# A float32 transformer block on one core: the same program with its SBUF operands moved apart modulo 512 bytes

## The chip, the cores and the metric

The kernel runs on one core of one Trainium2 chip. The metric is the device time of one execution in microseconds (us), as the median of several; smaller is better. Before the change the median of three executions is 741.97 us (741.67 to 742.17).

## The reference

The program is one layer of a streaming encoder for 512 frames of 1024 features, all in float32:

```
hn    = rms_norm(x) * norm1_g
proj  = hn @ w_in                      # [q_A k_A v_A | q_B k_B v_B | g_A g_B], 5120 wide
o_A   = softmax attention, 8 heads x 64, QK-norm, relative bias, all keys up to the frame's own 64-frame chunk
o_B   = stick-breaking attention, 8 heads x 64, strictly causal, no softmax
x     = x + (sigmoid(g_A) * (o_A @ w_branch_a) + sigmoid(g_B) * (o_B @ w_branch_b)) @ w_out
hid   = conv3(rms_norm(x) * norm2_g @ w_ffn_up) + conv_b     # causal, depthwise, 2 x 2816 wide
x     = x + (silu(hid[:, :2816]) * hid[:, 2816:]) @ w_ffn_down
```

## The kernel before

**Split products.** Every large product is made from two halves of each operand in the type that the profile calls fp32r: a high half (the cast of the number) and a low half (number minus high half). A product of two operands then takes three matmuls on TensorE: high by high, low by high and high by low. In the projections these are lines 188, 189 and 190 (`mm3`), in the first two projections line 306, in the down-projection lines 880, 881 and 882. Each matmul is two records in the profile: a weight load (PEld, 128x128, the stationary operand) and the matmul proper (PE, 256 or 512 columns of the moving operand). A row such as `pg<-hth,whi_up` names the output, then the moving operand, then the stationary one.

**Chunks of weights.** All weights of the projections come from HBM in chunks of 1 MB (128 partitions of 8 KB), those of the down-projection in chunks of 512 KB. `load` starts a chunk's transfer on the SP queue, into the tile `raw`, which has two places. `split_gen` then casts it on ScalarE into the tile `whi` (line 161) and subtracts on VectorE into the tile `wlo` (line 163); both tiles have two places too, so that chunk i+1 is split while TensorE works on chunk i (`run_chunk`). When a chunk is split, its raw place is free, and the chunk after the next is asked for at that point.

**The stages.** First the inputs and the first weights arrive and x is scaled and split into `hth` and `htl` (the transposed activations, 8 x 512 columns each); then the 24 projection chunks run with the two attentions between them; then the product with `w_out` and the second norm; then 22 up-projection chunks (48 matmuls of 512 columns each, in the first two chunks twice as many of 256; stationary `whi_up` or `wlo_up`, moving `hth` or `htl`), behind which the convolution, the gate and `pair_sums` prepare the down-projection's operands. The down-projection is a Strassen-like scheme of 7 products for each of 11 pairs of feature tiles and each half of the output columns. Its stationary operands are the 11 tiles `a`, eight of which lie in eight places with the tag `ap`; its moving operands are 256-column blocks of the weights' halves. Late weight chunks (`hl`) and the rows of x that are added at the end (`x_0`, `x_1`) take over places of `ap` whose operand is done.

**What sets the order.** The order of instructions on each engine is fixed when the program is built; engines wait for one another by semaphores. Tiles get fixed addresses at that time: each pool lays its places one behind the other along a partition, so the length of a tile decides where everything behind it begins.

**Where operands begin before.** In the program as built every matmul operand begins at a multiple of 512 bytes along its partition, with the one exception of a small column of row norms (line 280).

Of the kernel before, what the change touches and what calls it, by code (L numbers as in the profile page):

```python
# [8 lines left out]
F32 = mybir.dt.float32  # L9
F32R = mybir.dt.float32r  # L10
# [5 lines left out]
P = 128  # L16
S = 512
D = 1024
NT = S // P
# [45 lines left out]
def block_kernel(ctx: ExitStack, tc: tile.TileContext, x, xt, params, g2, rbx, wts, wdn, out):  # L65
# [6 lines left out]
    wp = ctx.enter_context(tc.tile_pool(name="wp", bufs=2))  # L72
# [30 lines left out]
    order = [key for key, _, _ in CHUNKS]  # L103

    raws, splits, late, ring = {}, {}, {}, []
    FIRST_DN = order.index("dn0_0")

    def load(i, parts=1):
        if i >= FIRST_DN:

            j = (i - FIRST_DN) % 3
            if i in (FIRST_DN, FIRST_DN + 2):
                ring.append(wp.tile([P, 2048], F32, tag="raw", name=f"raw_dn{len(ring)}"))
            raws[i] = ring[j // 2][:, j % 2 * 1024:(j % 2 + 1) * 1024]
            SP.dma_start(raws[i], wdn[i - FIRST_DN])
            yield
            return
        raws[i] = wp.tile([P, 2048], F32, tag="raw", name=f"raw_{order[i]}")
        n = 2048 // parts
        for j in range(parts):  # L120
            SP.dma_start(raws[i][:, j * n:(j + 1) * n], wts[i, :, j * n:(j + 1) * n])
            yield

    def down_sums(raw):

        b = raw.rearrange("p (b c) -> p b c", c=256)
        ts = ring[1][:, 1024:2048]
        t = ts.rearrange("p (b c) -> p b c", c=256)
        V.tensor_tensor(t[:, 0:2], b[:, 0:4:2], b[:, 0:2][:, ::-1], op=ALU.subtract)
        V.tensor_tensor(t[:, 2], b[:, 2], t[:, 0], op=ALU.subtract)  # L130
        ins = V.tensor_tensor(t[:, 3], t[:, 2], b[:, 3], op=ALU.subtract)

        late["halves"] = late.get("halves", ()) + (ins,)
        return ts

    def split_gen(i, pieces):

        if i >= len(order):
            return
        key = order[i]  # L140
        kn = CHUNKS[i][1]
        raw = raws.pop(i)
        if i < FIRST_DN + NP + 5:
            hi = wp.tile([P, 2048], F32R, tag="whi", name=f"whi_{key}")
            lo = wp.tile([P, 2048], F32R, tag="wlo", name=f"wlo_{key}")
        n = 2048 // pieces
        cuts = [(n * j, raw[:, n * j:n * (j + 1)]) for j in range(pieces)] if i < FIRST_DN else []
        if i >= FIRST_DN:

            if i < FIRST_DN + NP + 5:  # L150
                hi, lo = hi[:, 0:1792], lo[:, 0:1792]
            else:
                hl = late["pool"].tile([P, 3584], F32R, tag="ap", name=f"hl_{key}", bufs=8)
                hi, lo = hl[:, 0:1792], hl[:, 1792:3584]
            cuts, kn = [(0, raw[:, 256:1024]), (768, down_sums(raw))], 7
        splits[key] = (hi.rearrange("p (k c) -> p k c", k=kn), lo.rearrange("p (k c) -> p k c", k=kn))

        nxt = [i + 2] if i + 2 < FIRST_DN else [i + 2, i + 3] if i + 2 == FIRST_DN else [i + 3]
        for j, (o, src) in enumerate(cuts):
            sl = slice(o, o + src.shape[-1])  # L160
            cast = A.copy(hi[:, sl], src)  # L161
            E = G if i == 2 else V
            ins = E.tensor_tensor(lo[:, sl], src, hi[:, sl].bitcast(F32), op=ALU.subtract)  # L163
            if i >= FIRST_DN:

                late["halves"] = (behind(ins, late.get("halves", ())),)
                late["casts"] = (behind(cast, late.get("casts", ())),)
            if j == len(cuts) - 1:
                for n in nxt:
                    if n < len(order):  # L170
                        next(load(n))
            yield
# [3 lines left out]
    def run_chunk(key, body, pieces=4):  # L176

        sp = split_gen(pos[key] + 1, pieces)
        hi, lo = splits.pop(key)
        for _ in body(hi, lo):  # L180
            next(sp, None)
            yield
        for _ in sp:
            pass
# [29 lines left out]


    first = load(0, NK)
    for k in range(NK):
        SP.dma_start(xs[:, k, :], xt[k])
        next(first)
    for _ in load(1, 4):  # L220
        pass
# [31 lines left out]
    g1 = par[:, C_G1:C_G1 + NK]  # L253

    sp0 = split_gen(0, NK)
    for k in range(NK):
        A.activation(hth[:, k, :], xs[:, k, :], AF.Copy, scale=g1[:, k:k + 1])
# [284 lines left out]
    def behind(ins, others):  # L542

        for o in others:
            tc.add_manual_dep(ins.ins, o.ins.name, mybir.DependencyInfo(
                mybir.DependencyClass.NoSync, mybir.DependencyReason.DATA), reason="table order")
        return ins
# [104 lines left out]
    for s in range(len(steps)):  # L652
# [6 lines left out]
        br, h, t, e = pend.pop(0)  # L659
# [95 lines left out]
    hi, lo = splits.pop("wo3")  # L755
    sp = iter(())
    for y in wo_body(3)(hi, lo):
        if y == "split":
            sp = split_gen(pos["up0"], 4)
        next(sp, None)  # L760
# [3 lines left out]
    fp = late["pool"] = ctx.enter_context(tc.tile_pool(name="fp", bufs=1))  # L764
# [29 lines left out]
    def pair_sums(i):  # L794

        u0, u1 = ub[:, 2 * i % 4, :], ub[:, 2 * i % 4 + 1, :]
        lo_, hi_ = slice(0, 256), slice(256, 512)
        st = fp.tile([P, 768], F32, tag="st", name=f"st{i}", bufs=1)
        V.tensor_tensor(st[:, 0:256], u0[:, hi_], u1[:, hi_], op=ALU.add)
        V.tensor_tensor(u0[:, hi_], u0[:, lo_], u0[:, hi_], op=ALU.subtract)  # L800
        V.tensor_tensor(st[:, 256:512], st[:, 0:256], u0[:, lo_], op=ALU.subtract)
        V.tensor_tensor(st[:, 512:768], u1[:, lo_], st[:, 256:512], op=ALU.subtract)
        if i < 8:
            a = fp.tile([P, 3584], F32R, tag="ap", name=f"a{i}", bufs=8)
        else:
            a = cp.tile([P, 4096], F32R, tag=("xs", "hth", "htl")[i - 8], name=f"a{i}")
        pairs[i] = a
        for src, o, n in ((u0, 0, 512), (u1, 512, 512), (st, 1024, 768)):
            A.copy(a[:, o:o + n], src)
            V.tensor_tensor(a[:, 1792 + o:1792 + o + n], src, a[:, o:o + n].bitcast(F32), op=ALU.subtract)  # L810

    def up_fin(j, pg, pu, g=None):
        if g is None:
            g = gate(j, pg)
        u = ub[:, j % 4, :]
        conv(pu, NF + j, u)
        V.tensor_tensor(u, g, u, op=ALU.mult)
        if j % 2 == 1 and j // 2 < 9:
            pair_sums(j // 2)
# [29 lines left out]
    for i in (9, 10):  # L849
        pair_sums(i)  # L850
# [34 lines left out]
    def add(o, a, b, op=ALU.add, after=()):  # L885
        return behind(V.tensor_tensor(o, a, b, op=op), after)

    def blk(x, r, c):

        return x[:, 2 * r:2 * r + 2, 256 * c:256 * (c + 1)]  # L890
# [1 line left out]
    v3 = lambda ap: ap.rearrange("p (t c) -> p t c", t=2)  # L892

    def fetch(name, col):
        x = fp.tile([P, 3584], F32, tag="ap", name=name, bufs=8)[:, 0:2048].rearrange("p (t c) -> p t c", t=NT)
        for t in range(NT):
            SP.dma_start(x[:, t, :], x2d[t, :, col:col + 512])
        return x
# [22 lines left out]
    def rest0():  # L921

        c, u, v = tmp["c"], tmp["u"], tmp["v"]
        x = fp.tile([P, 3584], F32, tag="ap", name="x_0", bufs=8)[:, 0:2048].rearrange("p (t c) -> p t c", t=NT)
        get = lambda t: SP.dma_start(x[:, t, :], x2d[t, :, 0:512])
        for t, (o, i) in enumerate(((v3(u), blk(c, 1, 1)), (blk(c, 0, 1), v3(v)),
                                    (blk(c, 1, 1), v3(v)), (blk(c, 1, 0), v3(u)))):
            get(t)
            add(o, o, i, after=late["halves"])
            yield  # L930
        for t in range(NT):
            add(c[:, t, :], c[:, t, :], x[:, t, :], after=late["halves"])
            SP.dma_start(out[0, t * P:(t + 1) * P, 0:512], c[:, t, :])
            yield
# [49 lines left out]
    for s in range(2):  # L984
        for i in range(NP - 2 * s):
            if (s, i) == (0, 6):
                tmp["c"] = fp.tile([P, NT, S], F32, tag="ub", name="c_0")
            if (s, i) == (1, 1):
                rest = rest0()
            for _ in run_chunk(f"dn{s}_{i}", down_body(s, i)):  # L990
                pass

    for _ in split_gen(pos[f"dn1_{NP - 1}"], 2):
        pass
    tmp["x"] = fetch("x_1", 512)
    ends = [(i, splits.pop(f"dn1_{i}")) for i in (NP - 2, NP - 1)]
    prev = ()
# [54 lines left out]
```

## Time and profile before

| what | value |
|---|---|
| median of three executions | 741.97 us (741.67 to 742.17) |
| the profiled execution's own time | 742.19 us |
| its span, first to last instruction | 740.5 us |
| granted TensorE clock | 1.000 |
| TensorE busy, matmuls | 733.9 us, 4301 records |
| TensorE busy, weight loads | 651.9 us |
| VectorE, ScalarE, GpSimd busy | 538.0, 377.6 and 41.8 us |
| read from and written to HBM | 75.07 and 4.19 MB |

The span leaves 1.69 us of the profiled execution's own time outside (742.19 less 740.5). Busy times of PE overstate its work, since a matmul's record overlaps the next one's; how fast TensorE really goes is read from the distance between the starts of matmuls that follow one another, called pitch below.

### The profile page before, as it was taken

Reading aid. Unit: us, or ns where it says so; the run is one execution under the profiler, and the core shown is the slowest. Engines: PE = TensorE matmul, PEld = TensorE weight load, DVE = VectorE, ACT = ScalarE, POOL = GpSimd, SP = SyncE. Lnnn points to the kernel's source line nnn. Section 1 sums busy time; section 2 is a strip of 40 time slices with the busy share of each in tenths; the row PEclk is TensorE's granted clock in tenths of the full one; section 3 lists DMA queues with packets and bytes.
Section 4 is the critical chain, followed back from the end, with each engine's and each line's share of the span. In section 5 each row is a group of like instructions: output and inputs, shape, how many; then the busy total and the mean of one; then the engine's idle time right before and its main releaser. Section 6 shows DMA issues by size and latency. Waiting matters only on the chain.

```text
span 740.5 us, 10983 instructions
## 1 busy us (share of the span) xinstructions
PE 733.9 (99%) x4301; PEld 651.9 (88%) x4301; DVE 538.0 (73%) x984; ACT 377.6 (51%) x674; POOL 41.8 (6%) x73
## 2 busy tenths in 40 slices
PE   9999999999999999999999999999999999999997
PEld 8999998888988888888899888888888888999997
DVE  6578876775887888385275876766777676978895
ACT  6675655557766686353153554445355434434430
POOL 2701200000101111000000000000000000000000
PEclk9999999999999999999999999999999999999999
DMA  8632232211222112224332312322331321232552
GB/s 307 247 121 81 77 114 72 72 58 62 111 86 85 58 58 107 93 88 197 143 146 80 144 62 110 114 80 91 113 106 66 113 86 58 86 114 92 168 168 88
DMA packets 19205, 79.98 MB, mean 108 GB/s; under 512 B 2128, under 2 KB 4304, under 8 KB 13008
## 3 DMA queue, kind: packets, MB, share of 16 engines
q1 hardware_dynamic: 18864, 79.04, 30.5%
q8 instruction: 34, 0.56, 0.3%
q10 hardware_dynamic: 288, 0.23, 0.1%
q14 instruction: 19, 0.16, 0.1%
HBM read 75.07 MB, written 4.19 MB: 107 GB/s over the span
## 4 chain that ended last, share of the span: by engine, by line
PE 98%; DMA 1%; ACT 0%; DVE 0%; issue 0%; SPq 0%; DVEq 0%
PE pg L189 5%; PE pu L188 5%; PE pg L188 5%; PE pu L189 5%; PE pu L190 5%; PE pg L190 5%; PE P L882 5%; PE P L881 5%; PE P L880 5%; PE gA L188 2%; PE qkB L188 2%; PE gA L189 2%; PE gB L190 2%; PE qkB L190 2%; PE gB L188 2%; PE gA L190 2%
## 5 line engine op out<-in xcount | busy, mean ns | idle before, releaser
L163 DVE TENSOR_TENSOR wlo_up<-raw_up,whi_up 128x1024 fp32r<-128x1024 f32 (+1 forms) x50 | 52.4, 1094 | 49.4 <-ACT whi_up L161 49.4
L190 PE MATMUL pg<-hth,wlo_up 128*128 128x512 f32 (+1 forms) x192 | 71.5, 372 | 0.0
L189 PE MATMUL pu<-htl,whi_up 128*128 128x512 f32 (+1 forms) x192 | 71.5, 372 | 0.0
L188 PE MATMUL pg<-hth,whi_up 128*128 128x512 f32 (+1 forms) x192 | 71.4, 372 | 0.0
L188 PE MATMUL pu<-hth,whi_up 128*128 128x512 f32 (+1 forms) x192 | 71.4, 372 | 0.0
L189 PE MATMUL pg<-htl,whi_up 128*128 128x512 f32 (+1 forms) x192 | 71.4, 372 | 0.0
L190 PE MATMUL pu<-hth,wlo_up 128*128 128x512 f32 (+1 forms) x192 | 71.4, 372 | 0.0
L881 PE MATMUL P<-wlo_dn,a 128*128 128x256 f32 x224 | 62.2, 284 | 0.0
L882 PE MATMUL P<-whi_dn,a 128*128 128x256 f32 x224 | 62.1, 283 | 0.0
L880 PE MATMUL P<-whi_dn,a 128*128 128x256 f32 x224 | 59.1, 284 | 0.5 <-ACT whi_dn L161 0.5
L161 ACT CAST whi_up<-raw_up 128x1024 fp32r<-128x1024 f32 (+1 forms) x50 | 44.6, 948 | 29.2 <-PE pu L189 25.5
L161 ACT CAST whi_dn<-raw_dn 128x768 fp32r<-128x768 f32 (+1 forms) x32 | 29.0, 941 | 37.3 <-issue 22.3
L163 DVE TENSOR_TENSOR wlo_dn<-raw_dn,whi_dn 128x768 fp32r<-128x768 f32 (+1 forms) x32 | 34.8, 1091 | 15.1 <-ACT whi_dn L161 15.0
L881 PEld LDWEIGHTS P<-wlo_dn,a 128*128 128x128 f32 x224 | 43.1, 192 | 0.0
L882 PEld LDWEIGHTS P<-whi_dn,a 128*128 128x128 f32 x224 | 43.0, 192 | 0.0
L880 PEld LDWEIGHTS P<-whi_dn,a 128*128 128x128 f32 x224 | 41.0, 192 | 1.0 <-ACT whi_dn L161 0.9
L188 PEld LDWEIGHTS pu<-hth,whi_up 128*128 128x128 f32 x192 | 36.2, 189 | 6.3
L188 PEld LDWEIGHTS pg<-hth,whi_up 128*128 128x128 f32 x192 | 36.2, 189 | 6.3
L190 PEld LDWEIGHTS pu<-hth,wlo_up 128*128 128x128 f32 x192 | 36.2, 189 | 6.3
L190 PEld LDWEIGHTS pg<-hth,wlo_up 128*128 128x128 f32 x192 | 36.2, 188 | 6.3
L189 PEld LDWEIGHTS pu<-htl,whi_up 128*128 128x128 f32 x192 | 36.2, 189 | 6.1
L189 PEld LDWEIGHTS pg<-htl,whi_up 128*128 128x128 f32 x192 | 36.2, 189 | 6.1
(260 smaller groups left out, 2073.6 us busy)
## 6 DMA issues: line engine op xcount, KB each, us to landing
raw_up<-in_wts SPq DMA_DIRECT2D x22, 1024.0 KB, 4.7
raw_dn<-in_wdn SPq DMA_DIRECT2D x22, 512.0 KB, 3.3
raw_gA<-in_wts SPq DMA_DIRECT2D x4, 1024.0 KB, 4.7
raw_qkB<-in_wts SPq DMA_DIRECT2D x4, 1024.0 KB, 4.8
raw_gB<-in_wts SPq DMA_DIRECT2D x4, 1024.0 KB, 4.7
raw_wo<-in_wts SPq DMA_DIRECT2D x4, 1024.0 KB, 4.8
xs<-in_xt SPq DMA_DIRECT2D x8, 256.0 KB, 4.6
xtok<-in_x SPq DMA_DIRECT2D x4, 512.0 KB, 7.7
```

The source lines that it names most:

```text
L161: cast = A.copy(hi[:, sl], src)
L163: ins = E.tensor_tensor(lo[:, sl], src, hi[:, sl].bitcast(F32), op=ALU.subtract)
L188: PE.matmul(ps, sh, mh, start=first, stop=False)
L189: PE.matmul(ps, sh, ml, start=False, stop=False)
L190: PE.matmul(ps, sl, mh, start=False, stop=last)
L880: behind(PE.matmul(dst, sh, mh, start=first and t == 0, stop=False, skip_group_check=True), prev)
L881: PE.matmul(dst, sh, ml, start=False, stop=False, skip_group_check=True)
L882: prev = (PE.matmul(dst, sl, mh, start=False, stop=last, skip_group_check=True),)
```

## The change

Tiles are made longer than what they hold; the added bytes are never read or written. `raw` grows by 32 bytes per partition and place, `whi` and `wlo` by 64, the `ap` places by 64. All the slices that the program uses keep their lengths. The order of instructions on all engines, and the semaphores that they wait for, are the same in both built programs, row for row.

| tile | begins, bytes modulo 512, before | after |
|---|---|---|
| `raw`, two places | 0, 0 | 0, 32 |
| `whi`, two places | 0, 0 | 64, 128 |
| `wlo`, two places | 0, 0 | 192, 256 |
| `hth`, `htl`, `xs` (and the tiles that take their places) | 0 | 320 |
| tiles of the two attentions: `q`, `k`, `v`, probabilities, identity | 0 | 320 |
| `ap`, eight places | 0 (all) | 320, 256, 192, 128, 64, 0, 448, 384 |

```
-                ring.append(wp.tile([P, 2048], F32, tag="raw", name=f"raw_dn{len(ring)}"))
+                ring.append(wp.tile([P, 2056], F32, tag="raw", name=f"raw_dn{len(ring)}"))
...
-        raws[i] = wp.tile([P, 2048], F32, tag="raw", name=f"raw_{order[i]}")
+        raws[i] = wp.tile([P, 2056], F32, tag="raw", name=f"raw_{order[i]}")[:, 0:2048]
...
-            hi = wp.tile([P, 2048], F32R, tag="whi", name=f"whi_{key}")
-            lo = wp.tile([P, 2048], F32R, tag="wlo", name=f"wlo_{key}")
+            hi = wp.tile([P, 2064], F32R, tag="whi", name=f"whi_{key}")[:, 0:2048]
+            lo = wp.tile([P, 2064], F32R, tag="wlo", name=f"wlo_{key}")[:, 0:2048]
...
-                hl = late["pool"].tile([P, 3584], F32R, tag="ap", name=f"hl_{key}", bufs=8)
+                hl = late["pool"].tile([P, 3600], F32R, tag="ap", name=f"hl_{key}", bufs=8)
...
-            a = fp.tile([P, 3584], F32R, tag="ap", name=f"a{i}", bufs=8)
+            a = fp.tile([P, 3600], F32R, tag="ap", name=f"a{i}", bufs=8)
...
-        x = fp.tile([P, 3584], F32, tag="ap", name=name, bufs=8)[:, 0:2048].rearrange("p (t c) -> p t c", t=NT)
+        x = fp.tile([P, 3600], F32, tag="ap", name=name, bufs=8)[:, 0:2048].rearrange("p (t c) -> p t c", t=NT)
```

The two `x` lines (in `fetch` and in `rest0`) change alike.

More of the change, by code (lines that the diff above doesn't have):

```diff
@@ L923, in rest0 @@
         c, u, v = tmp["c"], tmp["u"], tmp["v"]
-        x = fp.tile([P, 3584], F32, tag="ap", name="x_0", bufs=8)[:, 0:2048].rearrange("p (t c) -> p t c", t=NT)
+        x = fp.tile([P, 3600], F32, tag="ap", name="x_0", bufs=8)[:, 0:2048].rearrange("p (t c) -> p t c", t=NT)
         get = lambda t: SP.dma_start(x[:, t, :], x2d[t, :, 0:512])
```

## The prediction

> **What bounds the kernel now.** I read the page's busy shares and chain of waits first, then the list of who waited on TensorE, then the timeline of the two long stages, to see what one matmul takes.
>
> ```profile
> PE 733.9 (99%) x4301; PEld 651.9 (88%) x4301; DVE 538.0 (73%) x984; ACT 377.6 (51%) x674; POOL 41.8 (6%) x73
> ...
> PE 98%; DMA 1%; ACT 0%; DVE 0%; issue 0%; SPq 0%; DVEq 0%
> ```
>
> ```profile
> PE warm L232 <- DVE warm L229: 1.5, 1, 1.5
> PE P L880 <- ACT whi_dn L161: 0.5, 2, 0.3
> PE qA L306 <- ACT whi_qA L161: 0.2, 1, 0.2
> PE gA L188 <- DVE mixA L441: 0.2, 1, 0.2
> ```
>
> The reader is to see that TensorE is the chain: 98% of it, and over the whole span it waited 2.4 us for other engines. So the change moves the time if it moves the pitch of the matmuls, the few us ahead of the first steady matmul, or the few behind the last one. What VectorE, ScalarE and the transfers gain or lose in between falls into slack, as long as it stays small.
>
> The pitch in the up-projection, first and last row of a run of 26 matmuls, with what the other engines did meanwhile:
>
> ```profile
> 470.20 0.39 PE L189 MATMUL pu<-htl,whi_up 128*128 128x512 f32 x1
> 470.43 0.39 PE L190 MATMUL pu<-hth,wlo_up 128*128 128x512 f32 x1
> ...
> 471.99 2.01 ACT L161 CAST whi_up<-raw_up 128x1024 fp32r<-128x1024 f32 x2 [2.07 <-PE pu L189]
> ...
> 473.07 2.36 DVE L163 TENSOR_TENSOR wlo_up<-raw_up,whi_up 128x1024 fp32r<-128x1024 f32 x2 [3.89 <-ACT whi_up L161]
> ...
> 475.46 0.33 SPq L121 DMA_DIRECT2D raw_up<-in_wts  x1
> ...
> 475.87 0.39 PE L190 MATMUL pg<-hth,wlo_up 128*128 128x512 f32 x1
> ```
>
> From 470.20 to 475.87 lie 25 pitches: 5.67 / 25 = 0.2268 us each. The down-projection, eleven matmuls of which I show the ends:
>
> ```profile
> 655.02 0.28 PE L881 MATMUL P<-wlo_dn,a 128*128 128x256 f32 x1
> 655.02 0.19 PEld L882 LDWEIGHTS P<-whi_dn,a 128*128 128x128 f32 x1
> 655.14 0.28 PE L882 MATMUL P<-whi_dn,a 128*128 128x256 f32 x1
> ...
> 656.22 0.28 PE L880 MATMUL P<-whi_dn,a 128*128 128x256 f32 x1
> ```
>
> 1.20 / 10 = 0.120 us each. From the two: 256 more columns cost 106.8 ns, so a column costs 0.417 ns, and 120 less 256 columns leaves a fixed part of 13 ns for each matmul, the same at 256 and at 512 columns.
>
> **The change part by part.** It adds no instruction and removes none; the order and the semaphores stay. What it moves are addresses, so each part is the question whether a duration depends on one.
>
> *TensorE's operands.* Before, the moving and the stationary operand of a matmul begin at the same place modulo 512; after it, 64 to 448 bytes apart in the projections, and in most of the down-projection. The attentions' own matmuls keep a common place. If the two streams, or TensorE and another engine, got in each other's way by address, the pitch should vary with what runs beside it. Three stretches of equal length in one up-projection chunk, with VectorE and ScalarE idle, with both at work, and with a weight transfer landing:
>
> ```profile
> 470.10:471.90 1.80, 1.80 (x10) 1.49 (x9) 0.00 (x0) 0.00 (x0) 0.00 (x0) 1.00 0.00 0
> 473.10:474.90 1.80, 1.80 (x9) 1.49 (x9) 1.80 (x2) 1.57 (x2) 0.00 (x0) 1.00 0.00 0
> 476.10:477.90 1.80, 1.80 (x9) 1.50 (x8) 1.70 (x3) 0.26 (x1) 0.00 (x0) 1.00 0.80 214
> ```
>
> (us, then busy time and count of PE, PEld, DVE, ACT and POOL, the clock, the share and GB/s of the transfers.) The weight loads, which are the shorter records and count cleanest, take 1.49 to 1.50 us in all three. So nothing outside TensorE slows it here. Against a collision of TensorE's two own streams the row says less, since they have been at the same distance in every matmul; but the fixed part is the same 13 ns where the moving operand is read for 107 ns (all of it beside a weight load) and where it is read for 213 ns (half of it beside one). I take zero for this part. The bounds: a gain of at most the fixed part down to what a weight load alone needs, and a loss of what a stall over one 64-byte step would be. The first from eight transposes, which have 128 columns and so wait for their weight loads alone; these rows are of the chain of waits:
>
> ```profile
> 1.69 4.88 DMA xs<-in_xt
> 6.60 0.73 ACT hth L257
> ...
> 8.50 9.86 PE qA L306 x80
> ...
> 97.19 0.87 PE qkT_A L396 x8
> ```
>
> 0.87 / 8 = 109 ns, 11 ns under the down-projection's pitch. 11 ns times 4301 matmuls is 47 us (a little too much, since the 128-column ones cannot gain). The loss: 64 bytes are 16 columns, 16 x 0.417 = 6.7 ns, times 4301 is 29 us. Both ends are kept as rivals. The zero is nearest to the windows' rows, which show no dependence on anything.
>
> [...]
>
> *VectorE and ScalarE.* Line 163 and line 161, the instructions that read or write most of the moved tiles:
>
> ```profile
> L163 DVE TENSOR_TENSOR wlo_up<-raw_up,whi_up 128x1024 fp32r<-128x1024 f32 x38 | 44.8, 1222 | 46.3 <-ACT whi_up L161 46.3
> L163 DVE TENSOR_TENSOR wlo_up<-raw_up,whi_up 128x512 fp32r<-128x512 f32 x12 | 7.6, 688 | 3.1 <-ACT whi_up L161 3.1
> L131 DVE TENSOR_TENSOR raw_dn<-raw_dn,raw_dn 128x256 f32<-128x256 f32 x15 | 6.4, 424 | 0.4
> L161 ACT CAST whi_up<-raw_up 128x1024 fp32r<-128x1024 f32 x38 | 38.1, 1053 | 23.8 <-PE pu L189 23.8
> ```
>
> 512 more elements cost 534 ns on VectorE, 256 more from 256 cost 264: a straight line of 1.04 ns an element, with no term that would depend on where operands lie. Zero. The cover if I am wrong: VectorE sat idle 46 us before these subtractions in the up-projection alone, ScalarE 24 before its casts; a tenth more on both (12 us over the stage) would fit in.
>
> *Transfers into moved places.* Every second `raw` now begins 32 bytes past a multiple of 512, `xs` 320 past, and what leaves at the end leaves from places 64 to 448 past. Median times to landing:
>
> ```profile
> raw_up<-in_wts SPq DMA_DIRECT2D x22, 1024.0 KB, 4.7
> raw_dn<-in_wdn SPq DMA_DIRECT2D x22, 512.0 KB, 3.3
> ...
> xs<-in_xt SPq DMA_DIRECT2D x8, 256.0 KB, 4.6
> ...
> tt<-in_rbx SPq DMA_DIRECT2D x8, 256.0 KB, 3.3
> ...
> out<-x SPq DMA_DIRECT2D x7, 128.0 KB, 1.9
> ```
>
> In the middle they are covered: a weight chunk is asked for when the split before it ends (475.46) and lands 4.7 us later, at 480.2. The place is split again two chunks after 471.99; the next split starts at
>
> ```profile
> 482.87 2.01 ACT L161 CAST whi_up<-raw_up 128x1024 fp32r<-128x1024 f32 x2 [0.42 <-PE pu L189]
> ```
>
> so a chunk takes 10.88 us and the place is needed at 493.75: 13.6 us of slack, nearly three landings. In the down-projection the ring has three places of 5 us each; the load of 3.3 us has about two chunks of cover too. Uncovered are the start, where the chain goes through one landing of `xs` (4.88 us), and the last transfer out (1.9 us). [...]
>
> The sum: 0 + 0 + 0 on the profiled execution's 742.19 us (span 740.5, 1.69 around it). That execution lies 0.22 us above the median of the runs shown, so I forecast **742.0 us**.
>
> **The rivals.**
>
> *The 13 ns are a collision of the two streams at the same place modulo 512, and moving them apart removes it.* For it: every operand pair before is at one place, so the trace cannot tell a collision from a fixed cost, and the floor of 109 ns shows that the weight load itself does not need 120. Against it: the same 13 ns at both lengths, steady to a nanosecond over whole stages, where a collision would be expected to depend on how the streams run past each other. Worth 11 ns x 4301 = 47 us at most: 742 - 47 = 695 us. A partial form (only the down-projection's eight places, 84 x 3 late matmuls and 672 earlier ones, 924 x 11 ns = 10 us) gives 732.
>
> *Landings at the start become slower.* The one place where a transfer decides is the first 8.5 us: TensorE's steady run begins at 8.50, behind the landing of `xs` at 6.57 and its cast and subtraction. The mechanism is a write to SBUF that no longer begins at a round address; each further us on that landing is one us at the end, and from 1.5 us on (a third of 4.88) it is a measurable loss. Half as long again, 2.4 us, gives 744.4; twice as long, 746.9. For it: all of `xs` and half of the `raw` places move off their round addresses at once, and `raw_kA`, queued there too, is at 32. Against it: a row of 2 KB or more is many times the shift. [...]
>
> *The streams stand apart now, and run into each other in mid-stretch.* This is the mirror image on the slower side: at a common start the weight load, which goes at half the moving stream's speed (109 ns for 128 columns against 53), stays behind it; from another start the faster one overtakes it. 6.7 ns x 4301 = 29 us: 771 us. Only that the pitches are insensitive to everything else speaks against it.
>
> *The change does not do what it says* in part: `raw` steps by 32, the halves of one `ap` tile keep a common place (7168 bytes is a multiple of 512), and some down-projection pairs still meet. This ends at 742 as well.
>
> **How the numbers follow.** A measurement of this kernel can tell about 0.2%, 1.5 us, from no change. No change by my working, with the part-way rival in it: 0.74. Collision removed, wholly or in part: 0.10. Landings slower by 1.5 us or more: 0.10. Streams colliding anew: 0.06. So faster 0.10, same 0.74, slower 0.16. The likeliest case alone would be 741.3 to 742.7; to leave no more than a fifth outside I go 2.5 us down (a slice of the collision) and 3 us up (the landing half as long again): 739.5 to 745.0.
>
> **What would show it.** The pitch of the up-projection at 227 ns and of the down-projection at 120 ns, the lines 161 and 163 at their times, `raw` landings at 4.7 and 3.3 us, the steady run beginning near 8.5 us: each step right. A pitch of 216 and 109 would prove the collision; one of 230 or more its mirror image; a steady run that begins past 10 us, with `xs` landing later, the transfers. I am wrong if any pitch moves by a nanosecond or more: one ns is 4.3 us.

## The result, and the profile after

| | before | after |
|---|---|---|
| median of three executions | 741.97 us (741.67 to 742.17) | 747.21 us (746.98 to 747.27) |
| span of the profiled execution | 740.5 us | 745.3 us |
| granted TensorE clock | 1.00 | 1.00 |

The change makes the kernel slower: ratio 1.007, 95% interval 1.0048 to 1.0093, 5.2 us. That lies outside the predicted range of 739.5 to 745.0.

TensorE is still the chain. Busy times and the shares of the chain of waits, after:

```profile
PE 737.9 (99%) x4301; PEld 648.3 (87%) x4301; DVE 538.0 (72%) x984; ACT 377.5 (51%) x674; POOL 42.0 (6%) x73
...
PE 95%; DMA 2%; DVE 1%; ACT 0%; SPq 0%; issue 0%; POOL 0%; DVEq 0%
```

Most of the 2% of DMA lie in the first 20 us: there the chain now passes through the landing of `xtok` and a wait of 0.2 us behind it (the last row of the waits below). VectorE and ScalarE work as long as before (538.0 and 377.5 us), TensorE's records are 4 us longer in sum. How fast it goes is read from counts in equal stretches. Before, two stretches in the up-projection and two in the down-projection (from:to and length in us, then busy time and count of PE, PEld, DVE, ACT and POOL, clock, share and GB/s of the transfers):

```profile
430.00:480.00 50.00, 50.00 (x223) 41.42 (x222) 37.00 (x53) 23.24 (x32) 0.00 (x0) 1.00 0.30 105
480.00:530.00 50.00, 50.00 (x222) 41.46 (x221) 35.77 (x49) 24.09 (x31) 0.00 (x0) 1.00 0.25 85
645.00:675.00 30.00, 30.00 (x252) 30.00 (x252) 24.20 (x33) 10.91 (x12) 0.00 (x0) 1.00 0.35 116
675.00:705.00 30.00, 30.00 (x252) 30.00 (x252) 25.67 (x38) 13.48 (x17) 0.00 (x0) 1.00 0.45 148
```

After, the same view:

```profile
430.00:480.00 50.00, 50.00 (x217) 40.64 (x216) 34.41 (x46) 22.74 (x29) 0.00 (x0) 1.00 0.25 87
480.00:530.00 50.00, 50.00 (x217) 40.67 (x217) 36.09 (x53) 23.29 (x31) 0.00 (x0) 1.00 0.28 103
645.00:675.00 30.00, 30.00 (x256) 30.00 (x255) 25.34 (x36) 12.06 (x13) 0.00 (x0) 1.00 0.33 108
675.00:705.00 30.00, 30.00 (x258) 30.00 (x257) 25.33 (x36) 13.55 (x17) 0.00 (x0) 1.00 0.43 142
```

A matmul's record is longer than the pitch, so a stretch holds about (its length + one record) / pitch of them. Up-projection: 50.39 / 223 = 0.226 us before, 50.39 / 217 = 0.232 after. Down-projection: 30.28 / 252 = 0.120 before, 30.28 / 256 = 0.118 and 30.28 / 258 = 0.117 after. So the change costs time in one stage and gives some back in the other. The timeline of the changed kernel says the same; first and last row of 26 matmuls in the up-projection and of eleven in the down-projection:

```profile
470.31 0.39 PE L188 MATMUL pu<-hth,whi_up 128*128 128x512 f32 x1
...
476.11 0.39 PE L189 MATMUL pg<-htl,whi_up 128*128 128x512 f32 x1
...
654.98 0.28 PE L881 MATMUL P<-wlo_dn,a 128*128 128x256 f32 x1
...
656.17 0.28 PE L881 MATMUL P<-wlo_dn,a 128*128 128x256 f32 x1
```

5.80 / 25 = 0.232 us, where it was 0.2268, and 1.19 / 10 = 0.119, where it was 0.120.

What else the prediction named stands still: the splits on VectorE and ScalarE by shape, the waits of TensorE, and the median landings, all after:

```profile
L163 DVE TENSOR_TENSOR wlo_up<-raw_up,whi_up 128x1024 fp32r<-128x1024 f32 x38 | 44.9, 1222 | 49.4 <-ACT whi_up L161 49.4
L161 ACT CAST whi_up<-raw_up 128x1024 fp32r<-128x1024 f32 x38 | 38.0, 1048 | 27.1 <-PE pu L189 27.1
```

```profile
PE warm L232 <- DVE warm L229: 1.5, 1, 1.5
PE P L880 <- ACT whi_dn L161: 0.5, 2, 0.3
PE qA L306 <- ACT whi_qA L161: 0.5, 1, 0.5
PE gA L188 <- DVE mixA L441: 0.2, 1, 0.2
PE rrow L280 <- POOL cols L273: 0.2, 1, 0.2
```

```profile
raw_up<-in_wts SPq DMA_DIRECT2D x22, 1024.0 KB, 4.8
raw_dn<-in_wdn SPq DMA_DIRECT2D x22, 512.0 KB, 3.3
...
xs<-in_xt SPq DMA_DIRECT2D x8, 256.0 KB, 4.6
```

1222 ns and 1048 ns against 1222 and 1053; waits of 2.9 us in all against 2.4; these three landings within 0.1 us of before. Some landings at the start differ by more, but so they do between runs: `xtok` took 7.7 us before and 8.3 after, 8.4 in E2, which moves no tile of that stage, and 7.3 in E1, which moves them all. The steady run begins no later either, 8.39 us against 8.50; this row is of the timeline after:

```profile
8.39 0.75 PE L306 MATMUL qA<-wlo_qA,hth 128*128 128x256 f32 x4
```

A ledger of the lateness shows where the 5 us arise: how much later than in before (+) or earlier (-) each stage starts. It is read from the start times of the two traces, so it holds for one execution of each. (The same ledger is given for the experiments below.)

| us against before, at the start of | after | E1 | E2 | E5 | E6 | E7 | E10 |
|---|---|---|---|---|---|---|---|
| the up-projection | +2.33 | -0.02 | +1.46 | +1.81 | -0.07 | -1.12 | -2.56 |
| its first chunk with 512 columns | +1.78 | -0.02 | +1.46 | +1.26 | -0.07 | -2.01 | -2.57 |
| the down-projection | +6.48 | -0.02 | +1.46 | +5.95 | -0.07 | -2.01 | -2.58 |
| the last matmul | +4.47 | -0.03 | -0.82 | +4.35 | -2.41 | -3.42 | -6.43 |
| whole span | +4.81 | +0.10 | -0.50 | +4.35 | -2.34 | -3.41 | -6.41 |

The 20 up-projection chunks with 512 columns cost 6.48 - 1.78 = 4.70 us, which is 4.9 ns on each of their 960 matmuls. The 924 matmuls of the down-projection, with 256 columns, gain 2.0 us, 2.2 ns each. The two up-projection chunks with 256 columns gain 0.55. The stages ahead, with both widths, lose 2.33, and there the two widths can be told apart too: the changed kernel is 0.59 us ahead at its first chunk with 512 columns, behind six chunks with 256, and loses 2.92 from there to the up-projection, a stretch in which all but two chunks have 512.

### The profile page after: what moved, and what is told of

Same layout as the page of the kernel before. It is cut to its first block, busy times and chain, and to the rows that moved or that the text cites. A ratio compares the mean times of both kernels' runs of the same rounds, so it can differ in the third digit from the quotient of the medians.

```text
span 745.3 us, 10983 instructions
## 1 busy us (share of the span) xinstructions
PE 737.9 (99%) x4301; PEld 648.3 (87%) x4301; DVE 538.0 (72%) x984; ACT 377.5 (51%) x674; POOL 42.0 (6%) x73
## 4 chain that ended last, share of the span: by engine, by line
PE 95%; DMA 2%; DVE 1%; ACT 0%; SPq 0%; issue 0%; POOL 0%; DVEq 0%
PE pu L190 6%; PE pg L190 5%; PE pu L189 5%; PE pg L189 5%; PE pg L188 5%; PE pu L188 5%; PE P L882 5%; PE P L881 5%; PE P L880 5%; PE gA L188 2%; PE qkB L188 2%; PE gA L190 2%; PE qkB L190 2%; PE gB L190 2%; PE gA L189 2%; PE wo L188 2%
## 5 line engine op out<-in xcount | busy, mean ns | idle before, releaser
L881 PE MATMUL P<-wlo_dn,a 128*128 128x256 f32 x224 | 61.5, 281 | 0.0
L882 PE MATMUL P<-whi_dn,a 128*128 128x256 f32 x224 | 61.5, 281 | 0.0
L881 PEld LDWEIGHTS P<-wlo_dn,a 128*128 128x128 f32 x224 | 42.2, 188 | 0.0
L882 PEld LDWEIGHTS P<-whi_dn,a 128*128 128x128 f32 x224 | 42.2, 189 | 0.0
L880 PEld LDWEIGHTS P<-whi_dn,a 128*128 128x128 f32 x224 | 40.2, 188 | 1.0 <-ACT whi_dn L161 0.9
```

The source lines that it names most:

```text
L880: behind(PE.matmul(dst, sh, mh, start=first and t == 0, stop=False, skip_group_check=True), prev)
L881: PE.matmul(dst, sh, ml, start=False, stop=False, skip_group_check=True)
L882: prev = (PE.matmul(dst, sl, mh, start=False, stop=last, skip_group_check=True),)
```

## The experiments

The theories. **Distance**: a matmul's pitch depends on how far its stationary operand begins from its moving one, modulo some power of two; what the change moves is this distance. **Own place**: each operand pays for not beginning at a multiple of 512 itself. **Others**: landings, or the splits, which write to moved places, slow TensorE through SBUF. From here on "distance" is the place of the stationary operand less that of the moving one, modulo 512. In before it is 0 for every large matmul. Pitches by distance are read from the start times in the traces, as means over one chunk (47 pitches with 512 columns, 41 with 256).

### E1: everything moved by the same 320 bytes

A tile that lies ahead of all others grows by 320 bytes, so that operands leave the multiples of 512 together, and all distances stay 0.

```
-    par = sm.tile([P, 224], F32, tag="par", name="par")
+    par = sm.tile([P, 304], F32, tag="par", name="par")
```

> The kernel before, with everything moved by the same 320 bytes (the parameter tile is longer), so that every operand begins at 320 modulo 512 and no two are apart. Theory 'distance' (the pitch is set by how far apart the columns that TensorE streams and the weights that it loads beside them lie): as before, 742.0 us, pitches 226.7 ns at 512 columns and 120.0 at 256. Rival 'own place' (an operand that does not begin at a multiple of 512 is read at another speed): as the changed kernel, 747 us, pitches about 231.6 and 118 ns.

Measured: 742.32 us, ratio 1.0001 (0.9991 to 1.0011). The windows of E1:

```profile
430.00:480.00 50.00, 50.00 (x222) 41.38 (x222) 37.01 (x53) 23.23 (x32) 0.00 (x0) 1.00 0.29 105
645.00:675.00 30.00, 30.00 (x252) 30.00 (x251) 24.21 (x33) 10.92 (x12) 0.00 (x0) 1.00 0.35 117
```

The counts are those of before (222 against 223, and 252), the landings come into moved places, and nothing changes. So own place falls, and so does any account by which leaving the multiple of 512 costs something by itself, as far as one shift, 320 bytes, can show it.

### E2: only the places of the down-projection's operands

The `ap` tiles grow to 3600 as in the change (the four lines with that tag); `raw`, `whi` and `wlo` stay. The projections' distances are 0, those of the down-projection step by 64.

```
-            a = fp.tile([P, 3584], F32R, tag="ap", name=f"a{i}", bufs=8)
+            a = fp.tile([P, 3600], F32R, tag="ap", name=f"a{i}", bufs=8)
```

> The kernel before, with only the eight operand places of the down-projection 64 bytes apart; weights and activations stay at 0 modulo 512. 'Distance': all stages of 512 columns as before at 226.7 ns, the 924 matmuls of the down-projection at some 118 ns in place of 120 on average, so about 740 us. 'Own place' (of the moving operand): the moving operand of the first 672 stays at 0, so 120 ns there, and only the 252 late ones can change; 741.5 to 742.0 us.

Measured: 740.62 us, ratio 0.9978 (0.9969 to 0.9988): this part of the change alone is a gain. Its windows:

```profile
430.00:480.00 50.00, 50.00 (x222) 41.42 (x221) 35.99 (x50) 23.62 (x31) 0.00 (x0) 1.00 0.28 98
645.00:675.00 30.00, 30.00 (x257) 30.00 (x257) 24.76 (x33) 11.98 (x13) 0.00 (x0) 1.00 0.33 111
```

The up-projection is as before (222), the down-projection faster (257 for 252). By the ledger its profiled execution had lost 1.46 us ahead of the up-projection, in stages in which no operand's distance differs (all of it in the first 34 us); from there to the last matmul it gained 2.28. So 1.5 us ahead of the up-projection can come from the start alone, and the first row of the ledger is read with that in mind.

### E5: only the weights' halves

`whi` and `wlo` grow by 64 bytes as in the change; `raw` and `ap` keep their lengths. All distances of the projections are those of the change (256 and 384, or 320 and 448), at other absolute places, and `raw` still begins at 0.

```
-            hi = wp.tile([P, 2048], F32R, tag="whi", name=f"whi_{key}")
-            lo = wp.tile([P, 2048], F32R, tag="wlo", name=f"wlo_{key}")
+            hi = wp.tile([P, 2064], F32R, tag="whi", name=f"whi_{key}")[:, 0:2048]
+            lo = wp.tile([P, 2064], F32R, tag="wlo", name=f"wlo_{key}")[:, 0:2048]
```

> The kernel before, with only the weights' halves 64 bytes apart (0, 64, 128, 192 modulo 512; the activations and all eight operand places end up together at 256, the raw places stay at 0). 'Distance': the matmuls of 512 columns lose as in the changed kernel, about 5 ns each in the up-projection, those of 256 columns gain 2 to 3 ns each; 747.5 us, a little above the changed kernel, which has the operand places too. If the moved raw places (transfers) were part of the loss, less than 747.

Measured: 746.84 us, ratio 1.0056 (1.0042 to 1.0069). Its windows:

```profile
430.00:480.00 50.00, 50.00 (x218) 40.62 (x217) 34.89 (x47) 22.75 (x29) 0.00 (x0) 1.00 0.25 87
645.00:675.00 30.00, 30.00 (x257) 30.00 (x256) 25.38 (x35) 12.08 (x13) 0.00 (x0) 1.00 0.36 113
```

The loss of the change is here, with every raw place where it was: 218 against 223 in the up-projection, and 5.95 - 1.26 = 4.69 us over its 20 chunks against 4.70 in the change. So the landings are out of it in this stage, although the time, 746.84, lies just under the 747 at which the expectation drew the line. The `raw` part was not run alone.

The other engines are out of it as well. A stretch of the changed kernel in which VectorE, ScalarE, GpSimd and the transfers do nothing, and the first and the last of the nine matmuls that start in it or just ahead or behind:

```profile
473.10:474.90 1.80, 1.80 (x9) 1.49 (x8) 0.00 (x0) 0.00 (x0) 0.00 (x0) 1.00 0.00 0
...
473.09 0.39 PE L188 MATMUL pu<-hth,whi_up 128*128 128x512 f32 x1
...
474.94 0.40 PE L190 MATMUL pu<-hth,wlo_up 128*128 128x512 f32 x1
```

1.85 / 8 = 0.231 us: the slower pitch is there with nothing beside TensorE. With E1, where the splits write to moved places at no cost (ratio 1.0001), the theory "others" falls.

### E3 and E4: a sweep over the distance

Each up-projection chunk from the third on, and each of the first 16 down-projection chunks, gets a distance of its own, the same for both halves; the six late chunks of the down-projection stay at 0. E4 has the same table of offsets but for two chunks, and a 96-byte tile ahead of `hth` (the last two lines, which E3 does not have), which shifts all distances and the places of the activations.

```
+OFFSETS = {'up2': (0, 16), 'up3': (0, 16), 'up4': (4, 20), 'up5': (4, 20), 'up6': (8, 24), 'up7': (8, 24),
...
+        oh, ol = OFFSETS.get(key, (0, 0))
...
+            hi = wp.tile([P, 2104], F32R, tag="whi", name=f"whi_{key}")[:, oh:oh + 2048]
+            lo = wp.tile([P, 2104], F32R, tag="wlo", name=f"wlo_{key}")[:, ol:ol + 2048]
...
+    gap = cp.tile([P, 24], F32, tag="gap", name="gap")
+    G.memset(gap, 0.0)
```

> One look at many distances in one kernel: in each up-projection chunk both halves of the weights lie at one distance ahead of the moving activations (which are all at 384 modulo 512), and that distance differs from chunk to chunk: 128 to 288 in steps of 16 or 32 in the even chunks from the third on, 352 to 480 and 0 in the odd ones; in the down-projection likewise with the roles changed. 'Distance': the pitch differs between chunks and is steady within one; the chunk at distance 0 has 226.7 ns, others between 216 and 236; some distances at 256 columns give 113 ns, some 120. 'Own place': the activations are at one place throughout, so all chunks of the up-projection have one pitch.

> The same as the first sweep, for distances 32 to 192 in the even chunks and 256 to 416 in the odd ones, with the activations at 480 modulo 512. 'Distance': where both sweeps have the same distance (128, 144, 160, 192, 256, 288, 352, 368, 384, 416) they have the same pitch within 1 ns although both operands lie elsewhere. 'Own place': they differ, or all chunks are alike.

Measured, one execution each: 749.24 and 750.17 us, beside a median of 742.3 for before. As wholes they are slow because most distances are bad for 512 columns. Two chunks that follow one another in E4 and hold 48 matmuls each show it; rows of its timeline, the first and the last matmul of the chunk at distance 32, then of the chunk at distance 256:

```profile
409.38 0.40 PE L192 MATMUL pg<-hth,whi_up 128*128 128x512 f32 x1
...
420.34 0.40 PE L194 MATMUL pu<-hth,wlo_up 128*128 128x512 f32 x1
420.58 0.39 PE L192 MATMUL pg<-hth,whi_up 128*128 128x512 f32 x1
...
431.25 0.40 PE L194 MATMUL pu<-hth,wlo_up 128*128 128x512 f32 x1
```

10.96 / 47 = 233.2 ns at 32, 10.67 / 47 = 227.0 ns at 256. All 512-column chunks of both sweeps, mean ns; the column's head is d, the rows are the distances d and d + 256:

| d | 0 | 16 | 32 | 48 | 64 | 80 | 96 | 112 |
|---|---|---|---|---|---|---|---|---|
| d | 226.7 | - | 233.3 | 233.3 | 233.4 | 232.0 | 234.2 | 233.2 |
| d + 256 | 227.2, 227.1 | 226.7 | 233.2, 233.2 | 233.3 | 233.4 | 232.1 | 234.3, 234.2 | 233.3, 233.4 |

| d | 128 | 144 | 160 | 176 | 192 | 208 | 224 | 240 |
|---|---|---|---|---|---|---|---|---|
| d | 232.2, 233.3 | 233.4, 233.4 | 233.4, 233.4 | 230.1 | 229.1, 228.8 | 231.8 | 233.3 | 227.1 |
| d + 256 | 233.3, 233.3 | 233.6 | 233.4, 233.2 | 230.2 | 233.3 | 231.8 | 233.3 | - |

Three things follow for 512 columns with one distance for both halves. The pitch is a function of the distance: where both sweeps have the same one (two values in the table), at other absolute places and in other chunks, they agree to about 1 ns. It repeats after 256 bytes to about 1 ns, 192 against 448 being the one exception. And it is 227 within 16 bytes of 0 or 256 and mostly 233.3 elsewhere: 6.7 ns more, which at the prediction's 0.417 ns a column is 16 columns, 64 bytes.

For 256 columns (41 pitches a chunk; all sweeps, E8 and E9 included) the picture is another: 119.9 at 0, 119.6 to 119.8 at 256, and elsewhere lower or about the same: 118.3 at 32, 117.8 at 64, 117.3 at 96, 116.9 at 112, 118.7 to 120.0 at 128, 120 at 152 and 160, 116.8 at 224 in one undisturbed chunk. Three distances stood out in the sweeps: 192 at 113.4, 320 at 113.6, and 144 at 114.6, which E6 and E7 left aside.

### E6: distance 192 in the whole down-projection

One unused tile of 192 bytes between the pools, nothing else; the projections keep distance 0.

```
+    gp = ctx.enter_context(tc.tile_pool(name="gp", bufs=1))
+    gap = gp.tile([P, 48], F32, tag="gap", name="gap")
+    G.memset(gap, 0.0)
```

> The kernel before, with one unused gap of 192 bytes ahead of the down-projection's tiles, and nothing else moved. 13 of its 22 chunks then have the stationary operand 192 bytes ahead of the moving one, and the last three late chunks 320 ahead; the others stay at 0. 'Distance', with the pitches of the sweeps (113.4 ns at 192 and 320, 120 at 0, for 256 columns): (546 + 126) x 6.6 ns = 4.4 us less, 737.6 us. If distance only trades one stage's time for another's: 742.

Measured: 740.03 us, ratio 0.9965 (0.9952 to 0.9979). The gain of the profiled execution, 2.34 us, is half of what 6.6 ns on each of the 672 earlier matmuls would give, 4.4. The windows say why:

```profile
645.00:675.00 30.00, 30.00 (x255) 30.00 (x255) 24.58 (x34) 10.92 (x12) 0.00 (x0) 1.00 0.38 123
675.00:705.00 30.00, 30.00 (x264) 30.00 (x264) 26.55 (x38) 14.20 (x18) 0.00 (x0) 1.00 0.43 142
```

In the first stretch the four chunks at distance 192 run at 117.8 ns, in the second the five at the same distance at 113.3; the rest of both are chunks at distance 0, at 120. Rows of the timeline, nine pitches at distance 192 in the first stretch and fifteen in the second:

```profile
655.44 0.28 PE L884 MATMUL P<-wlo_dn,a 128*128 128x256 f32 x1
...
656.50 0.28 PE L885 MATMUL P<-whi_dn,a 128*128 128x256 f32 x1
...
689.83 0.28 PE L885 MATMUL P<-whi_dn,a 128*128 128x256 f32 x1
...
691.53 0.28 PE L885 MATMUL P<-whi_dn,a 128*128 128x256 f32 x1
```

1.06 / 9 = 117.8 ns and 1.70 / 15 = 113.3 ns. So distance 192 has two steady rhythms for 256 columns. The first eight chunks take the slower one, the five that come behind three chunks at distance 0 the faster one. What decides between them is open: the last three chunks, at 320, also come behind chunks at distance 0, and take 117.8.

### E7: the best distance for each width

Chunks read with 512 columns go to distance 0 or 256, those with 256 columns to 192 or 320, in projections and down-projection; `OFFSETS` for all chunks, the code of E3, a gap of 32 bytes, `par` 8 columns shorter. The six late chunks of the down-projection stay at 0.

```
+OFFSETS = {'qA0': (24, 40), 'kA0': (0, 16),
...
+ 'up2': (40, 56), 'up3': (48, 0),
...
+ 'dn0_0': (24, 40), 'dn0_1': (0, 16),
...
```

> A kernel made from the sweeps: chunk by chunk the weights' halves begin at distance 0 or 256 from the other operand where matmuls have 512 columns, and at 192 or 320 where they have 256 (the q, k and v projections, the first two up-projection chunks, 16 of the 22 down-projection chunks). 'Distance': pitches 226.7 and 113.4 ns; 672 + 832 + 192 matmuls x 6.6 ns = 11.2 us less, 731 us; in the attention stage part of it may go to other waits, so 731 to 734. If not distance but its change within a stage matters: no better than the gap alone.

Measured: 738.93 us, ratio 0.995 (0.9937 to 0.9964). Faster than before, and well short of what was expected: the down-projection ran mostly at 118 ns, as in E6's first half. Its start times show where it left the faster rhythm: most of the third chunk ran at 113 ns, a short wait for weights came early in the fourth, and from there to the last early chunk the pitch was about 118.

### E8 and E9: what of the distance counts, and finer steps

In E8 six up-projection chunks have the high half at 0 or 256 and the low half at 320 or 64; the next six have the high half at 320 and the low half at 256. This asks whether a matmul pays for its own distance or for that of the weights which load while it streams (in before, L882's weight load and L881's matmul both begin at 655.02, and their records last 0.19 and 0.28 us). In the down-projection and the q, k and v projections E8 and E9 take the 256-column distances in finer steps, of 4 to 16 bytes for the most part.

```
...
+ 'up8': (40, 8), 'up9': (48, 16),
...
+ 'up14': (56, 56), 'up15': (0, 0),
...
+ 'dn0_0': (28, 44), 'dn0_1': (16, 32),
...
```

> One look. In the down-projection and the q, k, v projections the distance is stepped finely around the ones that were fast: 128 to 188 and 304 to 408 bytes, chunk by chunk. In up-projection chunks 8 to 13 the high halves lie at distance 0 or 256 and the low halves 64 further, in 14 to 19 the other way about; the rest is at 0 or 256. Order within a group of three: columns hth with weights hi, htl with hi, hth with lo. If what counts is the weights being loaded beside the running columns ('next'), in chunks 8 to 13 the matmul ahead of each lo is slow (233 ns) and the other two are at 226.7; if it is the weights already in place ('own'), the lo matmul itself is slow; if a disturbance carries over, two of three are slow (693 ns for three). For 256 columns: distances near 192 and 320 should be near 113 ns if the dependence is smooth, and scattered between 113 and 120 if it hangs on the rhythm in which a chunk is entered.

> One look. The same with distances 112 to 256 (192, 196, 200, 204 among them) and 320 to 456 bytes; all up-projection chunks of 512 columns at distance 0 or 256. 'Distance': chunks of 512 columns at 226.7 ns; at 256 columns 144 and 400 alike and 192 and 448 alike if the period is 256 bytes there too, as it is at 512 columns.

Measured, one execution each: 744.25 and 739.85 us, beside 742.35 for before. Two rows of E8, nine pitches apart, in a chunk with the low half alone at a bad distance:

```profile
489.93 0.39 PE L192 MATMUL pu<-hth,whi_up 128*128 128x512 f32 x1
...
492.01 0.39 PE L192 MATMUL pu<-hth,whi_up 128*128 128x512 f32 x1
```

2.08 / 9 = 231.1 ns. From each start to the next, the matmuls high by high, low by high and high by low take 228.3, 229.2 and 235.8 ns there, together 693.3. With the high half alone at a bad distance: 225.7, 236.0 and 231.7, together 693.4. Three undisturbed ones take 680. So one matmul in three at a bad distance costs 13.3 ns in all, and two in three cost the same: neither "its own distance" nor "that of the weights that load beside it" gives both. The third reading of the expectation, a disturbance that carries over to the next matmul, gives the 693 of the first six, but would make all three slow in the next six. This question stays open. What E8 does account for is the size of the loss in every second up-projection chunk of the changed kernel: these have the high half at 256 and the low half at 384, a good and a bad distance as here, and take 231.4 ns.

The fine steps found what E7 lacked. At distance 144 and 400 the down-projection's chunks of both runs went at 113 ns mostly (means 114.5 to 116.0), 8 bytes to either side at 120. At 192 the chunk of E9 took 118.0, where the sweep had 113.4.

### E10: 144 and 400 for the 256-column chunks

E7 with another table (256-column chunks at 144 or 400), a gap of 96 bytes, and `par` as in before.

```
+OFFSETS = {'qA0': (20, 36), 'kA0': (28, 44),
...
+ 'up2': (56, 8), 'up3': (0, 16),
...
+ 'dn0_0': (20, 36), 'dn0_1': (28, 44),
...
```

> As the kernel that sets the distance by width, but with 144 or 400 bytes for matmuls of 256 columns (the q, k and v projections, the first two up-projection chunks, 16 of the 22 down-projection chunks) and 0 or 256 for those of 512; the six late chunks stay at 0. 'Distance', with the pitches seen at 144 and 400 in every chunk so far (114.5 to 115.6 ns whatever came before): 672 x 5 + 192 x 5 + 832 x about 4 ns = 7.6 us less, 734.7 us. If the fast rhythm at 256 columns is a matter of how a chunk is entered even there: 738 to 739, as with 192 and 320.

Measured: 736.62 us, ratio 0.9919 (0.9906 to 0.9932): 6.0 us faster than before, and 10.6 us below the changed kernel's median. Its windows, and the ends of sixteen matmuls of its down-projection in the timeline:

```profile
430.00:480.00 50.00, 50.00 (x222) 41.44 (x221) 37.01 (x53) 23.39 (x31) 0.00 (x0) 1.00 0.30 106
645.00:675.00 30.00, 30.00 (x267) 30.00 (x266) 24.96 (x34) 12.83 (x15) 0.00 (x0) 1.00 0.36 113
675.00:705.00 30.00, 30.00 (x265) 30.00 (x264) 27.64 (x41) 13.17 (x16) 0.00 (x0) 1.00 0.49 160
```

```profile
654.83 0.28 PE L887 MATMUL P<-wlo_dn,a 128*128 128x256 f32 x1
...
656.53 0.28 PE L887 MATMUL P<-wlo_dn,a 128*128 128x256 f32 x1
```

222 in the up-projection, as before; 267 and 265 in the down-projection, where before had 252; 1.70 / 15 = 113.3 ns, the steady pitch of all 16 chunks. Here too waits for weights (0.8 us in the whole stage by its page: L886 0.6, L887 0.2) disturb the stream early in the third and the fourth chunk, but it falls back to 113.3 within some ten matmuls each time; in E7 it did so after the first such wait and not after the second. What is missing of the expectation (734.7) lies in part in the up-projection's two 256-column chunks: with 144 and 400 in the other role (weights stationary, activations moving) they stayed at 120 ns, where E7's 192 and 320 had gained 0.89 us (2.01 - 1.12 of the ledger). The late weight chunks, which lie in `ap` places beside the operands, keep distance 0 and 120.0 ns; what another distance is worth to their 252 matmuls was not tried with this table.

## Why the prediction was wrong

**TensorE is the chain, so the change moves the time if it moves the pitch of the matmuls.** Right. Of the 4.81 us by which the changed span is longer, 4.47 had come by the last matmul, with the pitch changed stage by stage; E1 and E5 leave nothing of it to VectorE, ScalarE or the landings that could be told from noise.

**"I take zero for this part" (TensorE's operands).** This step failed: a term put at nothing measured +4.9 ns on each 512-column matmul of the up-projection and -2.2 ns on each of the down-projection. The prediction had the reason in its hands: it says that the windows tell less of TensorE's own two streams, "since they have been at the same distance in every matmul". It then let these windows choose the value, because they were the nearest rows. They vary VectorE, ScalarE and the landings; the change varies the distance, which was one constant in the whole trace. A row in which the changed quantity never varies bounds nothing, however steady it is.

**"the fixed part is the same 13 ns" at both widths, taken as a sign that addresses don't enter.** The equality holds at distance 0 alone. With the column at 0.417 ns, the fixed part at 512 columns is 13 ns at 0 or 256 and 20 at most other distances; at 256 columns it is 13 at 0 and 6.7 at 144. These are 32, 48 and 16 columns' time. So the 13 ns are partly a matter of place after all, at least with 256 columns, where 6.7 of them went; with 512 no distance went under 13.

**The bounds.** The loss, 6.7 ns for a 64-byte step, is the full loss of the sweeps to a tenth of a nanosecond (233.4 against 226.7). That the two numbers agree is not evidence for a stall over one 64-byte step, which no run shows. The gain of 11 ns was too wide: the best seen is 120.0 to 113.3, also 6.7, and only at 256 columns. The pitches of 109 and 216 ns that the prediction names as the proof of the collision, 11 ns under 120 and 227, were reached by no run: the lowest chunk means are 113.3 and 226.6.

**The rivals.** "The streams stand apart now, and run into each other" had the right sign for the 512-column matmuls and the right price, at a chance of 0.06. It came to 5.2 us instead of 29 because the matmuls with 256 columns gain (2.2 ns each in the down-projection), because those of the attentions, which the 29 us count too, keep their distance, and because those with 512 lose 4.9 ns, not 6.7. Two halves at two distances in one chunk gave 231.4 ns (256 and 384) and 231.6 (320 and 448); the first is E8's case of one good and one bad half, the second stays unexplained, since the sweeps have 233.3 and more at either distance alone. The sign that the prediction set for this rival, a pitch of 230 or more, was met, but does not prove its story: that the loading stream overtakes the other one is not shown by any run. The collision that moving apart removes is half true, for 256 columns, where E10 draws its gain; its partial form at 732 took 11 ns for what is at most 6.7. "Landings at the start become slower" is refuted by E1, where `xs` and the `raw` places have moved (ratio 1.0001), and by the steady run's begin at 8.39 us. "The change does not do what it says" holds in its detail, since several pairs come to 0 or 256.

**VectorE, ScalarE, transfers at zero.** Right: 1222 and 1048 ns, 4.8, 3.3 and 4.6 us; what they vary by could not be told from noise. The third zero of the sum, for the transfers, was the author's estimate, which nothing in the trace of before shows; the runs have these landings within 0.1 us of before, and a ratio of 1.0001 in E1, where `xs` and the `raw` places have moved. The last transfers out, with rows of 1 KB (128 KB on 128 partitions), landed in 1.9 us before, and in 1.9 and 2.0 after.

**The test** that the prediction set itself ("I am wrong if any pitch moves by a nanosecond or more") found the error in the first windows. By the 0.2% bound the chance of slower was 0.16, mostly for the transfers, the wrong part.

## What to carry to other kernels

When a change varies something that was one constant in the profile, no steadiness of that profile prices it; measure it by itself first, here with an unused tile that shifts one operand against the other. In a stream of matmuls with a weight load each, place the stationary and the moving operand at a common place modulo 256 where the moving one has 512 columns (here 226.7 ns a matmul against 233.3 at most other distances), and try a distance of 144 or 400 where it has 256: here the down-projection gained from it (113.3 ns for 120.0), the two up-projection chunks did not (120). An average over mixed chunks, such as the 5.2 us here, can hide a loss and a gain.

## What the runs showed of the hardware

- In this kernel's streams of fp32r matmuls, each with its own weight load, the pitch depends on the distance of the two operands' places: 226.7 ns at 0 or 256 and 233.3 at most others, for 512 columns; 120.0 at 0 and 113.3 at 144 (in the down-projection), for 256. A common shift of 320 bytes does nothing (ratio 1.0001). The place of one operand against the other changes the pitch by 6.7 ns, so the two reads are not without effect on each other; by what means, no run tells.
- At distance 192, 256 columns have two steady rhythms, 113.3 and 117.8 ns, within one execution (E6). Why the stream came back to the faster one at 144 and 400 in every down-projection chunk tried (E10) is open, as is why the same distances with the roles changed did not have it, and which of the two reads gives way.
- Between the steps of 16 columns the sweep has values such as 229 and 231.8 that hold over a whole chunk. I have no account of them.
